# Other distances and pitches for the high and low parts of x, y and u in a two-layer encoder kernel

## The chip, the cores and the metric

The kernel runs on one core of one Trainium2 chip. The metric is the device time of one execution in microseconds; 2368.82 us is the median of three runs before the change (2368.69 to 2369.4). A second, profiled execution left the trace from which all rows below come.

## What is computed

Two encoder layers over 272 positions (256 tokens and 16 learned meta tokens) of width 2048. Each layer makes one wide projection, runs a gated linear attention and a neighbourhood attention side by side, projects their joined outputs back, and ends with a squared-ReLU MLP; two normalisations follow the two halves. Cut to its frame, the reference is:

```python
def _layer(h, w_in, ..., w_out, ln1_w, ln1_b, w_ff1, w_ff2, ln2_w, ln2_b):
    proj = jnp.einsum('bld,dp->blp', h, w_in)
    ...
    y_gla = _gla_mixer(gq, gk, gv, gr, glr, gla_w_up, gla_b_up, gla_norm_w)
    y_na = _na_mixer(nq, nk, nv, na_rel_bias).astype(h.dtype)
    mix = jnp.einsum('blm,md->bld', jnp.concatenate([y_gla, y_na], axis=-1), w_out)
    h = _layer_norm(DEEPNORM_ALPHA * h + mix, ln1_w, ln1_b)
    ff = jnp.einsum('blf,fd->bld', jnp.square(jax.nn.relu(jnp.einsum('bld,df->blf', h, w_ff1))), w_ff2)
    return _layer_norm(DEEPNORM_ALPHA * h + ff, ln2_w, ln2_b)
```

All is float32. Four products with weights carry nearly all the work: `w_in` (2048 x 6176), `w_out` (2048 x 2048), `w_ff1` (2048 x 8192) and `w_ff2` (8192 x 2048), in each layer.

## The kernel before

Each float32 factor is split into a high part, rounded to the matmul's float32r type, and a low part, which is what the rounding left. A product is made of three matmuls into one accumulator: high weights by high activations, high weights by low activations, and low weights by high activations. Positions are the columns of the moving operand, 128 channels at a time are the partitions. Layer 0 works on 272 positions; the last parts of layer 1 on 256.

**Activations.** A chunk is 128 channels of an activation, and a `Pair` (line 43) holds its two parts in one tile of the on-chip memory. `x` has 16 chunks and is the layer's input, `y` has 16 and is the attention's output. The MLP's hidden half, `u`, has 32 chunks: the first sixteen are laid over `y`'s tiles, the other sixteen (`u16` to `u31`) are in a pool of their own (line 788). A tile is `[P, 2, PITCH]`, PITCH = 288 elements: the high part starts at element 0 and the low part at 288, and the next chunk's tile follows 576 elements (2304 bytes) on. The tiles of `x` and `y` serve other uses at times: gate weights (line 373), the normalisation's rows and the outputs (`reuse`, line 938), the low part of the attention's values (line 294). Those read the tile as one flat row.

**Weights.** They stream from memory in tiles of 128 x 1024 (`made`, line 170): a DMA into `raw`, a copy on ScalarE to `wh` (line 178), a subtraction on VectorE to `wl` (line 179), each with three buffers. One tile holds eight stationary blocks of 128 x 128.

**Products.** `by_m` (line 248) makes one output tile of 128 channels at a time. For every eight chunks it calls `eight` (line 202), which multiplies them with one weight tile. Where there are 272 columns, line 214 gives for each chunk the high and then the low part to the same block of `wh`, sixteen matmuls, and line 217 then gives the eight high parts to `wl`. Where there are 256 columns (`once`), line 211 passes both parts of a chunk in one matmul of 2 x 256 columns, with an access pattern that jumps from the high part to the low part, eight matmuls, and line 217 follows with eight of 256 columns. A few products carry two columns more (258 and 274). `by_k` (line 228, matmuls in line 244) makes four or eight output tiles at once, two chunks at a time; it is used where chunks become ready one by one, and there the same part of a chunk is given to four blocks of weights running.

Matmuls run in the order in which they are issued. The rest of the work (gates, linear attention, neighbourhood attention, normalisation) is cut into generators, and `pump` (line 119) issues pieces of them between the products' groups. The change touches no order of this kind.

Of the kernel before, what the change touches and what calls it, by code (L numbers as in the profile page):

```python
# [7 lines left out]
F32 = mybir.dt.float32  # L8
F32R = mybir.dt.float32r
# [5 lines left out]
P = 128  # L15
D = 2048
DC = D // P
T = 256
# [4 lines left out]
GH, GDK, GDV = 4, 128, 256  # L23
# [14 lines left out]
MEET = 2  # L38
PAD = 40
PITCH = 288  # L40


class Pair(tuple):


    def __new__(cls, both):
        made = super().__new__(cls, (both[:, 0, :], both[:, 1, :]))
        made.both = both
        return made


class Trunk:
# [149 lines left out]
    def eight(self, ps, wh, wl, x, n, first, last, once):  # L202

        mm = self.nc.tensor.matmul
        c = lambda w, j: w[:, j * P:j * P + P]
        for j, v in enumerate(x):
            if once:  # L210
                mm(ps, lhsT=c(wh, j), rhs=v.both[:, :, :T], start=first and not j, stop=False)  # L211
                continue
            for i in range(2):
                mm(ps[:, :n], lhsT=c(wh, j), rhs=v[i][:, :n], start=first and not i + j, stop=False)  # L214
        o = ps[:, T:] if once else ps[:, :n]
        for j, (h, _) in enumerate(x):
            mm(o, lhsT=c(wl, j), rhs=h[:, :T if once else n], start=False, stop=last and j == 7)  # L217
# [55 lines left out]
        self.nc.vector.tensor_tensor(dst[low:low + n], src, dst[high[0]:high[0] + n].bitcast(F32), ALU.subtract)  # L273

    def pair(self, pool, name, c):
        return Pair(pool.tile([P, 2, PITCH], F32R, name=f"{name}{c}", tag=f"{name}{c}", bufs=1))


    def layer(self, l):
        nc, tc = self.nc, self.tc  # L280
        self.l = l
        self.full = l + 1 < DEPTH
        self.n = n = L if self.full else T
        with ExitStack() as actx:
            pool = lambda name, side, ctx=actx, bufs=1: ctx.enter_context(
                tc.tile_pool(name=name, bufs=bufs, side=side, reuse_waits="tile"))
            a = pool("att", "left")
            t = lambda nm, s: a.tile(s, F32, name=nm, tag=nm)
            self.qk = [t(f"qk{h}", [P, 2, L]) for h in range(GH)]
            for h in range(GH) if l else ():  # L290
                nc.gpsimd.memset(self.qk[h][:, 1, T:], 0.0)
            self.decay = [t(f"dec{h}", [P, 2, L]) for h in range(GH)]
            self.V = a.tile([P, 2 * GH, 2, P], F32R, name="V", tag="V")
            self.vlow = [self.pair(self.yp, "y", 12 + h).both.rearrange("p a c -> p (a c)") for h in range(GH)]
            self.VS = a.tile([80, GH * GDV], F32R, name="VS", tag="VS")
            nc.gpsimd.memset(self.VS.bitcast(F32), 0.0)
            self.y, self.gate, self.done, self.vt = [None] * DC, {}, set(), []
            if l:
                self.load_gates()
                self.by_m(self.x, [L + 2] * 4, lambda m, ps: self.fixed(self.ev_k, m, ps), pump=(1, NORMS[0]),  # L300
                          renew=True)
                first = self.by_k(self.x, L, self.normed)
                self.drain()
                self.lctx.close()
            with ExitStack() as ectx:
                self.ep = pool("early", "right", ectx)
                self.fcredit = 0
                self.fg.append(self.gates())
                if l == 0:
                    with ExitStack() as xctx:  # L310
                        self.xr = pool("xr", "right", xctx)
                        first = self.by_k(self.x, L, self.load_x, wide=True)
                    for m in range(4):
                        self.ev_k(m, first.pop(0))
                for m, ps in enumerate(first):
                    self.ev_v(m, ps)
                self.credit, self.alone = 0, True
                self.by_m(self.x, [n] * 4, self.ev_q, pump=(1, 1, True))
                self.by_m(self.x, [L] * 4, lambda m, ps: self.ev_v(4 + m, ps), pump=(1, 1, True))
                self.drain()  # L320
            self.a2 = pool("na", "left", bufs=2)
            with ExitStack() as gctx:
                self.credit = 0
                self.g2 = pool("gla", "right", gctx, 2)
                for h in range(GH):
                    self.bg.append(self.gla_head(h))
                for g in range(2):
                    self.by_m(self.x, [n] * 4, lambda m, ps: self.ev_r(4 * g + m, ps), pump=(1, GLA_R))
                self.na_tiles()
                for g in range(6):  # L330
                    if g == 5:
                        while self.bg:
                            self.step(self.bg, 1)
                        gctx.close()
                        self.ln_open()
                    ns = [n if (4 * g + m) % 3 == 0 else L for m in range(4)]
                    self.by_m(self.x, ns, lambda m, ps: self.ev_na(4 * g + m, ps), pump=(1, GLA_NA, True))
            self.alone = False
            ps = self.by_k(self.y, n, self.mixed)
            self.drain()  # L340
        self.tail(ps)
# [28 lines left out]

    def load_gates(self):

        place = lambda c: self.yp.tile([P, 2, PITCH], F32, name=f"gw{c}", tag=f"y{c}", bufs=1).rearrange("p a c -> p (a c)")[:, :512]
        *self.wup, self.wlr = (place(c) for c in (8, 9, 10))
        for d, w in enumerate(self.wup):
            self.nc.sync.dma_start(w[:LRK], self.i["wup"][self.l, :, d])
        self.nc.sync.dma_start(self.wlr, self.i["wlr"][self.l])
# [559 lines left out]

    def reuse(self, name, c, dtype):

        t = self.xp.tile([P, 2, PITCH], dtype, name=f"{name}{c}", tag=f"x{c}", bufs=1)  # L940
        return t.rearrange("p a c -> p (a c)")[:, :512]

    def affine(self, l, which, k):
        return tuple(self.vec[:, l, o:o + 1] for o in (32 * which + k, 32 * which + DC + k))
# [230 lines left out]
```

## Time and profile before

| what | value |
|---|---|
| median of three runs | 2368.82 us |
| profiled execution | 2369.49 us |
| its span | 2367.7 us |
| matmul instructions in the trace | 18180 |
| moved from memory | 414.03 MB |

The profile's page lists busy times by engine (PE is TensorE, PEld its weight load, DVE VectorE, ACT ScalarE, POOL GpSimd), slices of the span, the chain of work that ended last, and groups of instructions by line. In a group's row the fields are line, engine, operation, output tile and input tiles, shapes, count, then busy microseconds and the mean duration of one in nanoseconds, and behind the second bar the idle time before it with its releaser. A row of the timeline gives the start, the time that the merged instructions cover, and their count. Matmuls overlap: the time that one costs is the distance to the next one's start, and not its duration.

### The profile page before, as it was taken

Reading aid. Unit: us, or ns where it says so; the run is one execution under the profiler, and the core shown is the slowest. Engines: PE = TensorE matmul, PEld = TensorE weight load, DVE = VectorE, ACT = ScalarE, POOL = GpSimd, SP = SyncE. Lnnn points to the kernel's source line nnn. Section 1 sums busy time; section 2 is a strip of 40 time slices with the busy share of each in tenths; the row PEclk is TensorE's granted clock in tenths of the full one; section 3 lists DMA queues with packets and bytes.
Section 4 is the critical chain, followed back from the end, with each engine's and each line's share of the span. In section 5 each row is a group of like instructions: output and inputs, shape, how many; then the busy total and the mean of one; then the engine's idle time right before and its main releaser. Section 6 shows DMA issues by size and latency. Waiting matters only on the chain.

```text
span 2367.7 us, 44607 instructions
## 1 busy us (share of the span) xinstructions
PE 2359.4 (100%) x18180; PEld 2241.3 (95%) x18180; DVE 1520.6 (64%) x2432; ACT 1220.3 (52%) x2100; POOL 136.0 (6%) x200
## 2 busy tenths in 40 slices
PE   9999999999999999999999999999999999999998
PEld 9999999999999999999999899999988888888888
DVE  5588777775544455546576887778765455666654
ACT  5666664564433344444456666655644333444443
POOL 0021100100000000000030111101100000000000
PEclk9999999999999999999999999999999999999999
DMA  8555545555555556555555555456666666667664
GB/s 259 154 161 153 156 136 175 173 176 178 178 178 174 176 177 178 178 178 177 175 183 173 164 162 163 153 162 187 188 191 187 188 187 188 188 189 218 188 187 143
DMA packets 118301, 419.02 MB, mean 177 GB/s; under 512 B 13512, under 2 KB 14024, under 8 KB 118096
## 3 DMA queue, kind: packets, MB, share of 16 engines
q1 hardware_dynamic: 117808, 415.65, 57.7%
q8 instruction: 142, 2.33, 0.4%
q10 hardware_dynamic: 288, 0.52, 0.1%
q14 instruction: 63, 0.52, 0.1%
HBM read 414.03 MB, written 2.10 MB: 176 GB/s over the span
## 4 chain that ended last, share of the span: by engine, by line
PE 98%; DVE 1%; issue 0%; ACT 0%; POOL 0%; DVEq 0%; ACTq 0%; POOLq 0%
PE mm L214 35%; PE mm L217 29%; PE mm L211 22%; PE mm L244 6%; PE bg L244 1%; PE bg L754 1%; PE mm L693 1%; PE bg L554 0%; PE bg L400 0%; DVE wl L179 0%; PE mm L719 0%; PE mm L443 0%; PE bg L880 0%; PE bg L605 0%; PE bg L635 0%
## 5 line engine op out<-in xcount | busy, mean ns | idle before, releaser
L179 DVE TENSOR_TENSOR wl<-raw,wh 128x1024 fp32r<-128x1024 f32 (+1 forms) x768 | 941.9, 1227 | 625.3 <-ACT wh L178 622.2
L178 ACT CAST wh<-raw 128x1024 fp32r<-128x1024 f32 (+1 forms) x768 | 804.6, 1048 | 926.5 <-PE mm L214 381.2
L214 PE MATMUL mm<-x,wh 128*128 128x272 f32 (+2 forms) x4224 | 569.7, 287 | 0.0
L214 PEld LDWEIGHTS mm<-x,wh 128*128 128x128 f32 x4224 | 541.0, 188 | 0.8 <-PE mm L693 0.2
L217 PE MATMUL mm<-x,wl 128*128 128x272 f32 (+3 forms) x3264 | 466.3, 285 | 0.0
L217 PEld LDWEIGHTS mm<-x,wl 128*128 128x128 f32 x3264 | 436.9, 188 | 12.7
L211 PE MATMUL mm<-x,wh 128*128 128x512 f32 x1152 | 292.1, 396 | 0.0
L211 PEld LDWEIGHTS mm<-x,wh 128*128 128x128 f32 x1152 | 207.5, 189 | 38.4 <-PE mm L693 0.4
L217 PE MATMUL mm<-y,wl 128*128 128x272 f32 (+1 forms) x1408 | 200.0, 284 | 0.0
L217 PEld LDWEIGHTS mm<-y,wl 128*128 128x128 f32 x1408 | 189.0, 188 | 7.4
L214 PE MATMUL mm<-y,wh 128*128 128x272 f32 (+1 forms) x1440 | 193.3, 286 | 0.0
L214 PEld LDWEIGHTS mm<-y,wh 128*128 128x128 f32 x1440 | 184.3, 188 | 0.0
L211 PE MATMUL mm<-y,wh 128*128 128x512 f32 x688 | 174.3, 395 | 0.0
L217 PE MATMUL mm<-u,wl 128*128 128x272 f32 (+1 forms) x1024 | 145.4, 284 | 0.0
L211 PEld LDWEIGHTS mm<-y,wh 128*128 128x128 f32 x688 | 123.9, 189 | 22.4
L217 PEld LDWEIGHTS mm<-u,wl 128*128 128x128 f32 x1024 | 137.5, 188 | 5.4
L214 PE MATMUL mm<-u,wh 128*128 128x272 f32 (+1 forms) x1056 | 141.2, 286 | 0.0
L214 PEld LDWEIGHTS mm<-u,wh 128*128 128x128 f32 x1056 | 134.8, 188 | 0.0
L211 PE MATMUL mm<-u,wh 128*128 128x512 f32 x496 | 125.4, 395 | 0.0
L211 PEld LDWEIGHTS mm<-u,wh 128*128 128x128 f32 x496 | 89.4, 189 | 16.3
L244 PE MATMUL mm<-x,wh 128*128 128x272 f32 (+1 forms) x512 | 73.5, 289 | 0.0
L244 PEld LDWEIGHTS mm<-x,wh 128*128 128x128 f32 x512 | 68.0, 191 | 0.0
(273 smaller groups left out, 1857.2 us busy)
## 6 DMA issues: line engine op xcount, KB each, us to landing
raw<-in_wff SPq DMA_DIRECT2D x512, 512.0 KB, 3.6
raw<-in_win SPq DMA_DIRECT2D x190, 512.0 KB, 3.9
raw<-in_wout SPq DMA_DIRECT2D x64, 512.0 KB, 3.7
nb<-in_nab SPq DMA_DIRECT2D x16, 352.0 KB, 5.7
xraw<-in_xT SPq DMA_DIRECT2D x7, 272.0 KB, 4.7
out<-out SPq DMA_DIRECT2D x5, 256.0 KB, 3.2
brow<-in_norm SPq DMA_DIRECT2D x4, 256.0 KB, 4.9
gw<-in_wup SPq DMA_DIRECT2D x4, 196.0 KB
```

Of the source, the lines that this page charges most:

```text
L178: nc.scalar.copy(wh[:, c], raw[:, c])
L179: self.wl = nc.vector.tensor_tensor(wl[:, c], raw[:, c], wh[:, c].bitcast(F32), ALU.subtract).ins
L211: mm(ps, lhsT=c(wh, j), rhs=v.both[:, :, :T], start=first and not j, stop=False)
L214: mm(ps[:, :n], lhsT=c(wh, j), rhs=v[i][:, :n], start=first and not i + j, stop=False)
L217: mm(o, lhsT=c(wl, j), rhs=h[:, :T if once else n], start=False, stop=last and j == 7)
L244: self.nc.tensor.matmul(ps[g + m][:, :n], lhsT=parts[p][0][:, c:c + P], rhs=acts[k + j][parts[p][1]][:, :n], start=k + j + p == 0, stop=k ...
L693: nc.tensor.matmul(ps[hh][:, t * NKEY:t * NKEY + NKEY], lhsT=q[hs, NM + t * P:NM + t * P + P], rhs=k[hs, t, :], start=True, stop=True)
L754: nc.tensor.matmul(po[t][hs, :P], lhsT=v2[ts, hs] if rest else v1[:, t, hs], rhs=p2[ts, hh, :] if rest else p1[:, 2 * hh + t, :], start=re ...
```

## The change

Every group of tiles gets a distance between high and low part and a pitch of its own, in elements:

| tiles | distance, pitch before | distance, pitch after | in bytes after |
|---|---|---|---|
| x | 288, 576 | 288, 592 | 1152, 2368 |
| y (and u0 to u15) | 288, 576 | 288, 608 | 1152, 2432 |
| u16 to u23 | 288, 576 | 272, 576 | 1088, 2304 |
| u24 to u31 | 288, 576 | 320, 640 | 1280, 2560 |
| sp (sums of the normalisations) | 288, 576 | 288, 576 | 1152, 2304 |

The tile becomes one flat row; a `Pair` takes its parts as slices of it and makes the two-part view of line 211 once (`once`). The larger tiles need some 5 KB more on each partition, and the scratch for DMA descriptors goes from 8192 to 2048 bytes a partition.

```diff
+LAYOUT = {"x": (288, 592), "y": (288, 608), "u": (272, 576), "v": (320, 640), "sp": (288, 576)}
...
-    def __new__(cls, both):
-        made = super().__new__(cls, (both[:, 0, :], both[:, 1, :]))
-        made.both = both
+    def __new__(cls, flat, low):
+        width = min(low, flat.shape[-1] - low)
+        made = super().__new__(cls, (flat[:, :width], flat[:, low:low + width]))
+        made.flat, made.once = flat, flat[:, :2 * low].rearrange("p (a c) -> p a c", a=2)[:, :, :T]
         return made
...
-                mm(ps, lhsT=c(wh, j), rhs=v.both[:, :, :T], start=first and not j, stop=False)
+                mm(ps, lhsT=c(wh, j), rhs=v.once, start=first and not j, stop=False)
...
     def pair(self, pool, name, c):
-        return Pair(pool.tile([P, 2, PITCH], F32R, name=f"{name}{c}", tag=f"{name}{c}", bufs=1))
+        low, whole = LAYOUT["v" if name == "u" and c > 23 else name]
+        return Pair(pool.tile([P, whole], F32R, name=f"{name}{c}", tag=f"{name}{c}", bufs=1), low)
...
-            self.vlow = [self.pair(self.yp, "y", 12 + h).both.rearrange("p a c -> p (a c)") for h in range(GH)]
+            self.vlow = [self.pair(self.yp, "y", 12 + h).flat for h in range(GH)]
...
-        place = lambda c: self.yp.tile([P, 2, PITCH], F32, name=f"gw{c}", tag=f"y{c}", bufs=1).rearrange("p a c -> p (a c)")[:, :512]
+        place = lambda c: self.yp.tile([P, LAYOUT["y"][1]], F32, name=f"gw{c}", tag=f"y{c}", bufs=1)[:, :512]
...
-        t = self.xp.tile([P, 2, PITCH], dtype, name=f"{name}{c}", tag=f"x{c}", bufs=1)
-        return t.rearrange("p a c -> p (a c)")[:, :512]
+        return self.xp.tile([P, LAYOUT["x"][1]], dtype, name=f"{name}{c}", tag=f"x{c}", bufs=1)[:, :512]
...
-    nc = bacc.Bacc("TRN2", target_bir_lowering=False, num_devices=1, dynamic_dma_scratch_size=8192)
+    nc = bacc.Bacc("TRN2", target_bir_lowering=False, num_devices=1, dynamic_dma_scratch_size=2048)
```

Below, a chunk's "place" is the byte address of a part's first column within a partition, modulo 256.

## The prediction

> **What bounds the kernel now.** I read the page's first part, then the chain of waits, then the timeline of TensorE (PE).
>
> ```profile
> span 2367.7 us, 44607 instructions
> PE 2359.4 (100%) x18180; PEld 2241.3 (95%) x18180; DVE 1520.6 (64%) x2432; ACT 1220.3 (52%) x2100; POOL 136.0 (6%) x200
> PEclk9999999999999999999999999999999999999999
> PE 98%; DVE 1%; issue 0%; ACT 0%; POOL 0%; DVEq 0%; ACTq 0%; POOLq 0%
> PE mm L214 35%; PE mm L217 29%; PE mm L211 22%; PE mm L244 6%; PE bg L244 1%; PE bg L754 1%; PE mm L693 1%; PE bg L554 0%; PE bg L400 0%; DVE wl L179 0%; PE mm L719 0%; PE mm L443 0%; PE bg L880 0%; PE bg L605 0%; PE bg L635 0%
> L179 DVE TENSOR_TENSOR wl<-raw,wh 128x1024 fp32r<-128x1024 f32 (+1 forms) x768 | 941.9, 1227 | 625.3 <-ACT wh L178 622.2
> ```
>
> PE is idle for 2367.7 - 2359.4 = 8.3 us, at full granted clock in every slice, and four lines of matmuls (214, 217, 211, 244) are 93% of the chain. VectorE, which makes the low halves of the weights, stands idle 625 us waiting for ScalarE's high halves. So the kernel's time is the spacing from one matmul's start to the next, times their number, and nothing else moves it by much. A duration in the groups (287 ns) is no spacing, since matmuls overlap; the spacings come from the starts in the timeline. First layer 0, then layer 1:
>
> ```profile
> 600.63 1.16 PE L217 MATMUL mm<-x,wl 128*128 128x272 f32 x8
> 601.63 2.14 PE L214 MATMUL mm<-x,wh 128*128 128x272 f32 x16
> 603.61 1.16 PE L217 MATMUL mm<-x,wl 128*128 128x272 f32 x8
> 604.61 1.65 PE L214 MATMUL mm<-x,wh 128*128 128x272 f32 x12
> ```
> ```profile
> 2000.40 2.02 PE L211 MATMUL mm<-x,wh 128*128 128x512 f32 x8
> 2002.26 1.11 PE L217 MATMUL mm<-x,wl 128*128 128x256 f32 x8
> 2003.21 1.09 PE L211 MATMUL mm<-x,wh 128*128 128x512 f32 x4
> ```
>
> L214: (603.61 - 601.63) / 16 = 123.75 ns for 272 columns. L217: (604.61 - 603.61) / 8 = 125.0 ns for 272 columns, (2003.21 - 2002.26) / 8 = 118.75 ns for 256. L211: (2002.26 - 2000.40) / 8 = 232.5 ns for 2 x 256. The change alters nothing but where these matmuls' moving operands lie, so I ask whether the place shows in a spacing.
>
> **What place does so far.** In bytes the old distance is 1152 = 4 x 256 + 128 and the old pitch 2304 = 9 x 256. So every high part starts at the same place of 256 bytes (call it 0) and every low part at 128. L214 reads high, low, high, low (0, 128, 0, 128); L217 reads eight high parts, always starting at 0. L244 reads one chunk's part four times running, and another group reads from other places altogether: lines 635 to 637 read pieces of a packed tile whose starts lie 1088 = 4 x 256 + 64 bytes apart. From the chain of waits in order of time, and from the timeline:
>
> ```profile
> 494.24 24.10 PE mm L244 x192
> 1680.23 22.83 PE mm L244 x192
> ```
> ```profile
> 312.12 0.29 PE L636 MATMUL bg<-parts,V 128*128 128x272 f32 x1
> ...
> 313.64 0.29 PE L639 MATMUL bg<-am,VS 80*128 80x272 f32 x1
> ```
> ```profile
> 600.63 0.28 PE L217 MATMUL mm<-x,wl 128*128 128x272 f32 x1
> ...
> 600.75 0.54 PE L217 MATMUL mm<-x,wl 128*128 128x272 f32 x3
> ...
> 600.88 0.54 PE L217 MATMUL mm<-x,wl 128*128 128x272 f32 x3
> ```
>
> L244 makes 24.10 / 192 = 125.5 ns at 272 columns, 22.83 / 192 = 118.9 ns at 256. The mixed places make (313.64 - 312.12) / 12 = 126.7 ns (twelve spacings between first and last row). So at 272 columns repeating a start costs 125.0 to 125.5, alternating 0 and 128 costs 123.75: some 1.75 ns. At 256 columns there is no such difference. Within one L217 group single spacings differ: 600.63 to 600.75 is 120 ns, 600.75 to 600.88 is 130 ns. The same instruction on the same kind of tile can be 10 ns cheaper, so there is something to win, and 120 ns is the best that these rows show.
>
> The floor lies lower. The kernel's first four real matmuls are (5.46 - 4.55) / 4 = 228 ns apart:
>
> ```profile
> 4.55 1.11 PE L244 MATMUL mm<-x,wh 128*128 128x272 f32 x4
> 5.46 0.66 PE L244 MATMUL mm<-x,wl 128*128 128x272 f32 x2
> ```
>
> If the array runs there at half its later rate, 114 ns would be the price of the columns alone (an estimate), and 10 of the 123.75 ns would be overhead. The Trainium skill's page "TensorE: Matmul & The Clock Gate", section "Back-to-back issue gap", gives N/2.4 + 2.5 ns for a warm matmul, 115.8 ns at 272 columns; the trace's 123.75 is 8 ns above that, and by that rule alone no choice of addresses would be worth anything.
>
> **The change part by part.** The instructions of each engine stay the same in number, form and order; addresses move. The counts, by form:
>
> ```profile
> L214 PE MATMUL mm<-x,wh 128*128 128x272 f32 x3584 | 483.0, 287 | 0.0
> L211 PE MATMUL mm<-x,wh 128*128 128x512 f32 x1152 | 292.1, 396 | 0.0
> L217 PE MATMUL mm<-x,wl 128*128 128x272 f32 x1792 | 260.3, 287 | 0.0
> L214 PE MATMUL mm<-y,wh 128*128 128x272 f32 x1408 | 189.2, 286 | 0.0
> L211 PE MATMUL mm<-y,wh 128*128 128x512 f32 x688 | 174.3, 395 | 0.0
> L217 PE MATMUL mm<-x,wl 128*128 128x256 f32 x1152 | 159.8, 281 | 0.0
> L214 PE MATMUL mm<-u,wh 128*128 128x272 f32 x1024 | 137.1, 286 | 0.0
> L211 PE MATMUL mm<-u,wh 128*128 128x512 f32 x496 | 125.4, 395 | 0.0
> L217 PE MATMUL mm<-y,wl 128*128 128x272 f32 x704 | 102.3, 287 | 0.0
> L217 PE MATMUL mm<-y,wl 128*128 128x256 f32 x704 | 97.7, 281 | 0.0
> L217 PE MATMUL mm<-x,wl 128*128 128x274 f32 x192 | 28.2, 289 | 0.0
> L217 PE MATMUL mm<-x,wl 128*128 128x258 f32 x128 | 18.0, 283 | 0.0
> ```
>
> In the built program x, y and u lie at different multiples of 256 bytes, yet their groups of one form agree within 1 ns, so I count places modulo 256 alone. The new places are: x high 0, 64, 128, 192 from chunk to chunk, low 128 further; y high 0, 128, 0, 128, low 128 further; the first eight chunks of u high 0, low 64; the last eight high 0 and low 0.
>
> *L217 and its 274- and 258-column kin, on x and y:* consecutive starts no longer repeat. No row has a run of starts that all step by 64 or 128. Bounds: 120 ns (best single spacing) and 126.7 ns (mixed places). I take the middle between 125.0 and 120, 122.5 ns, since the best spacings occur in this very form: -2.5 ns x (1792 + 704 + 192 + 128 = 2816) = -7.0 us; bounds -14.1 and +4.8 us. At 256 columns repetition cost nothing, so 0 for 1152 + 704; bounds 1 ns either way, 1.9 us. On u the high parts still repeat: 0.
>
> *L211:* on x and y a matmul no longer starts where its forerunner did: -2.5 ns x (1152 + 688 = 1840) = -4.6 us. For u, where the jump to the low part also becomes 64 or 0 instead of 128, I take 0. Bounds: two separate 256-column matmuls, 237.5 ns, which is +5.0 ns; and 256 columns more at the slope of L217, (125.0 - 118.75) / 16 = 0.39 ns, which is 218.7 ns or -13.8. For 2336 matmuls that is +11.7 to -32 us.
>
> *L214:* on x each start still differs from the one before: 0. On y the low part of a chunk and the high part of the next now start at the same place, so half of 1408 pay the repetition: 704 x 1.75 = +1.2 us. On the first eight of u: 0. On the last eight every start repeats: 512 x 1.75 = +0.9 us. Bounds for 6016 matmuls: 120 ns, -22.6 us, and 126.7 ns, +17.7 us.
>
> *L244:* four matmuls running read the same part, so starts repeat as before: 0, bounds 1.75 ns on about 960, 1.7 us either way.
>
> *Everything else* costs nothing. ScalarE and VectorE write the parts at other addresses under PE's cover; the first would have to grow by the 625 us that VectorE waits to be felt. The scratch for descriptors that shrinks is used by no queue here (all are hardware queues):
>
> ```profile
> q1 hardware_dynamic: 117808, 415.65, 57.7%
> q10 hardware_dynamic: 288, 0.52, 0.1%
> ```
>
> Sum: -7.0 - 4.6 + 1.2 + 0.9 = -9.5 us. The profiled execution took 2369.49 us (span 2367.7 and 1.8 around it), so 2360.0; it is 0.7 above the median of 2368.82, so **2359 us** for a median. If PE gains 9.5 us, the weights must come 0.4% faster; VectorE's wait shows room, so no other engine is late next.
>
> **The rivals.** *Slower.* A 272-column stream ends 64 bytes past its starting place (1088 = 4 x 256 + 64). In L214 every next stream now begins 64 bytes beyond that end, after high as after low; that relation, and not alternation as such, may make the 123.75. After the change it survives only for high to low in x and y. If the rest fall to the mixed 126.7, L214 as a whole loses up to 17.7 us, and L217 and L211, which go from one untuned relation to another, give half of my gain, 5.8: +11.9, about 2381 us. It decides from 11.6 / 6016 = 1.9 ns per L214 matmul on. For it: L214 is the cheapest of the four groups at 272 columns, and that relation is what it has to itself. Against it: the 126.7 was measured on a tile that the built program puts 32 bytes off a multiple of 64, which no new place is.
>
> *Nothing.* Every old and new distance is a multiple of 64 bytes. If only the place within 64 matters, nothing changes: 2369 us. For it: at 256 columns all groups make 118.75 to 118.9. Against it: 123.75 beside 125.0. The Trainium skill's page "SBUF — State Buffer", section "Who interferes with whom", says the same more strongly: PE and ScalarE "never wait on anyone" and the moving operand and the weights have a read port each. By that rule the time stays; 120 and 130 ns within one group of rows speak against it.
>
> *Much faster.* All 272-column matmuls reach 120 ns and L211 loses the same 3.5 ns: -14.1 - 22.6 - 8.2 = -45 us, 2324 us. For it: 120 ns occurs. Against it: groups average it away everywhere today.
>
> **How the numbers follow.** Forecast 0.51, slower 0.27, nothing 0.12, much faster 0.10. The forecast's own range, half the way to each bound, the terms added as independent, is 2340 to 2372. The range that holds 8 in 10 goes from 2333, short of the much faster case, to 2382, the slower one. About 0.2%, 4.7 us, is what a measurement tells from no change. Faster by more: 0.10 and most of 0.51, together 0.58; within: 0.12 and 0.03 of the forecast's edge, 0.15; slower: 0.27.
>
> **What would show it.** Right: L217 at 272 columns on x near 122.5 ns where it was 125.0, L211 on x near 230, L214 on x still 123.75, on the last eight of u 125.5. Wrong: L217 on x at 125 or above; L214 on x at 125 or more (then the slower rival); all groups as before (nothing). A PE idle for more than 8.3 us would show that something other than spacings moved.

## The result and the profile after

The changed kernel takes 2372.93 us (median of 20 runs) where the one before takes 2369.03 (20 runs beside them): a ratio of 1.0016, interval 1.001 to 1.0022. It is 3.9 us slower, inside the 0.2% that was set as no change, but clear of the noise, and on the other side from the forecast of 9.5 us faster. The profile's page of the changed kernel; code lines lie two further down, and three from line 277 to line 939:

```profile
span 2371.1 us, 44606 instructions
PE 2362.8 (100%) x18180; PEld 2242.4 (95%) x18180; DVE 1520.3 (64%) x2432; ACT 1219.3 (51%) x2100; POOL 136.4 (6%) x200
PEclk9999999999999999999999999999999999999999
PE mm L216 35%; PE mm L219 29%; PE mm L213 22%; PE mm L246 6%; PE bg L246 1%; PE bg L757 1%; PE mm L696 1%; PE bg L557 0%; PE bg L403 0%; DVE wl L181 0%; PE mm L722 0%; PE mm L446 0%; PE bg L883 0%; PE bg L608 0%; PE bg L638 0%
L181 DVE TENSOR_TENSOR wl<-raw,wh 128x1024 fp32r<-128x1024 f32 (+1 forms) x768 | 941.9, 1227 | 628.3 <-ACT wh L180 627.1
```

TensorE is idle for 2371.1 - 2362.8 = 8.3 us, as before, at full granted clock, with the same chain and the same count of matmuls. The 3.4 us that the span grew are all in the spacings of matmuls. From the timeline of the changed kernel, x in layer 0, then in layer 1, then u and y in layer 0 (start, time covered, line, count); the last block is u and y before the change:

```profile
601.42 1.16 PE L219 MATMUL mm<-x,wl 128*128 128x272 f32 x8
602.41 2.15 PE L216 MATMUL mm<-x,wh 128*128 128x272 f32 x16
604.40 1.16 PE L219 MATMUL mm<-x,wl 128*128 128x272 f32 x8
605.39 0.78 PE L216 MATMUL mm<-x,wh 128*128 128x272 f32 x5
```
```profile
2000.21 1.10 PE L219 MATMUL mm<-x,wl 128*128 128x256 f32 x8
2001.15 2.03 PE L213 MATMUL mm<-x,wh 128*128 128x512 f32 x8
2003.02 1.10 PE L219 MATMUL mm<-x,wl 128*128 128x256 f32 x8
```
```profile
644.19 2.16 PE L216 MATMUL mm<-u,wh 128*128 128x272 f32 x16
646.19 1.17 PE L219 MATMUL mm<-u,wl 128*128 128x272 f32 x8
647.19 2.17 PE L216 MATMUL mm<-u,wh 128*128 128x272 f32 x16
649.20 1.16 PE L219 MATMUL mm<-u,wl 128*128 128x272 f32 x8
650.20 2.17 PE L216 MATMUL mm<-y,wh 128*128 128x272 f32 x16
652.21 1.16 PE L219 MATMUL mm<-y,wl 128*128 128x272 f32 x8
```
```profile
643.35 2.14 PE L214 MATMUL mm<-u,wh 128*128 128x272 f32 x16
645.33 1.16 PE L217 MATMUL mm<-u,wl 128*128 128x272 f32 x8
646.33 2.14 PE L214 MATMUL mm<-u,wh 128*128 128x272 f32 x16
648.31 1.16 PE L217 MATMUL mm<-u,wl 128*128 128x272 f32 x8
649.31 2.14 PE L214 MATMUL mm<-y,wh 128*128 128x272 f32 x16
651.29 1.16 PE L217 MATMUL mm<-y,wl 128*128 128x272 f32 x8
```

On x, in the groups shown, L219 at 272 columns falls from 125.0 to (602.41 - 601.42) / 8 = 123.75 ns and at 256 from 118.75 to (2001.15 - 2000.21) / 8 = 117.5; L213 rises from 232.5 to (2003.02 - 2001.15) / 8 = 233.75; L216 rises from 123.75 to (604.40 - 602.41) / 16 = 124.4. On the first eight of u L216 takes (646.19 - 644.19) / 16 = 125.0, on the last eight and on y (652.21 - 650.20) / 16 = 125.6; before, L214 took (645.33 - 643.35) / 16 = 123.75 on all three. Gains and losses of one nanosecond nearly cancel. Over the whole trace, each matmul's distance to the next start, averaged by line (numbers of before), tiles and columns:

```
line tiles columns   count   before  after ns   sum of differences us
211  x     2x256      1152   233.23  234.23    +1.15
211  y     2x256       688   232.49  232.77    +0.20
211  u16-23, u24-31    496   232.50  233.43, 230.10   +0.23, -0.59
214  x     272        3584   124.61  125.05    +1.61
214  y     272        1408   123.94  125.59    +2.32
214  u16-23, u24-31   1024   123.73  125.12, 125.41   +0.70, +0.88
217  x     272        1792   126.02  125.20    -1.47
217  y     272         704   125.09  124.97    -0.08
217  x     256        1152   119.45  118.42    -1.19
217  y     256         704   118.40  117.10    -0.92
217  u16-23, u24-31 256  512   118.37  119.64, 119.10   +0.33, +0.18
all others                                     -0.05
sum                                            +3.3
```

(The averages of x hold the few waits at the start of a product, which are nearly the same before and after.)

### The profile page after: what moved, and what is told of

Read it like the earlier page. It is cut to its first block, busy times and chain, and to the rows that moved or that the text cites. A ratio compares the mean times of both kernels' runs of the same rounds, so it can differ in the third digit from the quotient of the medians.

```text
span 2371.1 us, 44606 instructions
## 1 busy us (share of the span) xinstructions
PE 2362.8 (100%) x18180; PEld 2242.4 (95%) x18180; DVE 1520.3 (64%) x2432; ACT 1219.3 (51%) x2100; POOL 136.4 (6%) x200
## 4 chain that ended last, share of the span: by engine, by line
PE 98%; DVE 1%; issue 0%; ACT 0%; POOL 0%; DVEq 0%; ACTq 0%; POOLq 0%
PE mm L216 35%; PE mm L219 29%; PE mm L213 22%; PE mm L246 6%; PE bg L246 1%; PE bg L757 1%; PE mm L696 1%; PE bg L557 0%; PE bg L403 0%; DVE wl L181 0%; PE mm L722 0%; PE mm L446 0%; PE bg L883 0%; PE bg L608 0%; PE bg L638 0%
## 5 line engine op out<-in xcount | busy, mean ns | idle before, releaser
L216 PE MATMUL mm<-x,wh 128*128 128x272 f32 (+2 forms) x4224 | 571.2, 287 | 0.0
L216 PEld LDWEIGHTS mm<-x,wh 128*128 128x128 f32 x4224 | 541.3, 188 | 0.8 <-PE mm L696 0.2
L219 PE MATMUL mm<-x,wl 128*128 128x272 f32 (+3 forms) x3264 | 464.0, 284 | 0.0
L219 PEld LDWEIGHTS mm<-x,wl 128*128 128x128 f32 x3264 | 434.7, 188 | 13.1
L213 PE MATMUL mm<-x,wh 128*128 128x512 f32 x1152 | 293.3, 396 | 0.0
L213 PEld LDWEIGHTS mm<-x,wh 128*128 128x128 f32 x1152 | 206.7, 188 | 39.6 <-PE mm L696 0.4
L219 PE MATMUL mm<-y,wl 128*128 128x272 f32 (+1 forms) x1408 | 199.0, 283 | 0.0
L216 PE MATMUL mm<-y,wh 128*128 128x272 f32 (+1 forms) x1440 | 195.6, 287 | 0.0
L219 PEld LDWEIGHTS mm<-y,wl 128*128 128x128 f32 x1408 | 188.2, 188 | 7.5
L216 PEld LDWEIGHTS mm<-y,wh 128*128 128x128 f32 x1440 | 186.3, 188 | 0.0
L213 PE MATMUL mm<-y,wh 128*128 128x512 f32 x688 | 174.4, 395 | 0.0
L219 PE MATMUL mm<-u,wl 128*128 128x272 f32 (+1 forms) x1024 | 146.1, 285 | 0.0
L213 PEld LDWEIGHTS mm<-y,wh 128*128 128x128 f32 x688 | 123.1, 188 | 22.9
L219 PEld LDWEIGHTS mm<-u,wl 128*128 128x128 f32 x1024 | 138.3, 189 | 5.4
L216 PE MATMUL mm<-u,wh 128*128 128x272 f32 (+1 forms) x1056 | 142.8, 287 | 0.0
L216 PEld LDWEIGHTS mm<-u,wh 128*128 128x128 f32 x1056 | 136.1, 188 | 0.0
L213 PE MATMUL mm<-u,wh 128*128 128x512 f32 x496 | 125.0, 394 | 0.0
L213 PEld LDWEIGHTS mm<-u,wh 128*128 128x128 f32 x496 | 89.0, 188 | 16.3
```

Source lines behind the costliest of these rows:

```text
L213: mm(ps, lhsT=c(wh, j), rhs=v.once, start=first and not j, stop=False)
```

## The experiments

All run the reference's computation but for the three that are named. "Spacing" is as above, start to next start, from each run's own trace.

### One group of tiles at a time

```diff
-LAYOUT = {"x": (288, 592), "y": (288, 608), "u": (272, 576), "v": (320, 640), "sp": (288, 576)}
+LAYOUT = {'x': (288, 592), 'y': (288, 576), 'u': (288, 576), 'v': (288, 576), 'sp': (288, 576)}
```

and in the same way for y, for the first eight own chunks of u, and for the last eight.

> x alone gets the new pitch (288, 592); y and u keep 288, 576; the descriptor scratch is small as in the changed kernel. Theory A (the spacing of a matmul depends on the places of its own group's starts modulo 256 bytes): only the spacings of x move, as they did in the changed kernel: 272 columns in L216 124.6 to 125.05 ns, in L219 down by 0.8 ns, 256 columns down by 1 ns, 2 x 256 up by 1 ns; sum of the differences about 0, so 2369. Theory B (something that all groups share, the smaller scratch or the shift of everything behind it, makes the change): about +3.9 us here too, 2373, and y and u slower though their distances are old.

> y alone gets (288, 608). Theory A: y at 272 columns in L216 goes from 123.9 to 125.6 ns (1408 matmuls, +2.3 us), y at 256 in L219 from 118.4 to 117.1 (-0.9), 2 x 256 +0.2: +1.5 us, 2370.5; x and u as before. Theory B: about 2373 with x and u changed.

> The first eight own chunks of u alone get (272, 576). Theory A: their 512 matmuls at 272 columns in L216 go from 123.75 to 125.1 ns (+0.7 us), 256 columns +0.3, 2 x 256 +0.2: +1.3 us, 2370.3; the last eight as before. Theory B: about 2373.

> The last eight chunks of u alone get (320, 640). Theory A: 272 columns in L216 123.7 to 125.4 (+0.9 us), 256 columns +0.2, 2 x 256 from 232.5 to 230.1 (-0.6): +0.5 us, 2369.5, inside the noise; the four kernels' differences add up to the whole change. Theory B: about 2373.

Measured beside one set of runs before (2369.13 us): x 2369.38 (ratio 1.0001, 0.9992 to 1.001), y 2370.93 (1.0009, 1.0 to 1.0018), the first eight of u 2370.99 (1.0008, 0.9999 to 1.0017), the last eight 2370.57 (1.0007, 0.9998 to 1.0016). Single ratios hardly leave the noise; the spacings do, since a group that a run leaves alone repeats closely: with x alone, no group of y or u on these three lines moved by more than 0.03 us in all. With y alone, x (old places) and then y (new places), from the timeline:

```profile
601.46 2.14 PE L216 MATMUL mm<-x,wh 128*128 128x272 f32 x16
603.44 1.16 PE L219 MATMUL mm<-x,wl 128*128 128x272 f32 x8
...
649.21 2.17 PE L216 MATMUL mm<-y,wh 128*128 128x272 f32 x16
651.22 1.15 PE L219 MATMUL mm<-y,wl 128*128 128x272 f32 x8
```

x keeps (603.44 - 601.46) / 16 = 123.75 ns, y has (651.22 - 649.21) / 16 = 125.6 as in the changed kernel. Summed over each trace, the spacings' differences are -0.4 us (x), +1.3 (y), +2.3 (first eight), +1.3 (last eight), 4.5 together, and the medians' differences 0.25 + 1.8 + 1.86 + 1.44 = 5.35, where the whole change has 3.3 and 3.9.

Theory B falls: no single group brings the whole change, and with x alone y and u stay. Theory A holds for x, and only in part for the others: a group also changes its neighbours. With y alone, untouched L216 of the first eight of u goes from 123.75 to 125.0 ns (+0.6 us), and with the last eight alone, untouched L216 of y from 123.94 to 124.52 (+0.8 us). With the first eight alone, their own L216 goes to 126.0 ns, where the whole change has 125.1, and the untouched last eight go from 123.7 to 124.2; that is most of why the first eight cost 2.3 us and not the expected 1.3, and y's +0.8 is why the last eight cost 1.3 and not 0.5. All are products over 32 chunks, in which y and u follow each other. Effects of this size are enough for the four not to add up.

### Other addresses, the same places

```diff
-LAYOUT = {"x": (288, 592), "y": (288, 608), "u": (272, 576), "v": (320, 640), "sp": (288, 576)}
+LAYOUT = {'x': (288, 576), 'y': (288, 576), 'u': (352, 704), 'v': (352, 704), 'sp': (288, 576)}
```

> All sixteen own chunks of u get distance 352 and pitch 704 (1408 = 5 x 256 + 128 and 2816 = 11 x 256 bytes): other addresses, the old places modulo 256. Theory A (places modulo 256 alone): every spacing of u as before, 272 columns in L216 123.7 ns, 2 x 256 232.5, 256 columns 118.4; 2369. Rival C (the distance itself or a larger modulus counts): u's spacings move by 1 to 2 ns as with (272, 576) and (320, 640), +1 to +3 us.

2368.97 us beside 2369.01 (ratio 1.0, 0.9991 to 1.0009), and the sum of spacings of u moved by 0.00 us. For u's old places, then, neither the distance as such nor the address beyond 256 bytes counts; the smaller scratch, which this kernel has too, does not either. C falls here.

### Matmuls alone

A kernel of its own with 32 matmuls running per block and a fixed step between starts (the `one` below), blocks parted by one short matmul; then blocks of 2 x 256 columns with a distance and a step. The encoder is left out; the output is a copy of the input.

```python
ONE = [(n, step, twice, wp) for n, steps in ((272, (1280, 1344, 1152, 1216, 1088)), (256, (1280, 1344, 1152, 1216, 1024)))
       ...
def one(nc, ps, w, m, n, at, j, wp, k):
    nc.tensor.matmul(ps[:, :n], lhsT=w[:, wp + j * P:wp + j * P + P], rhs=m[:, at:at + n], start=not k, stop=k == REP - 1)
```

> Matmuls alone, no other engine at work: 32 running with one step between starts, then the next step; the encoder is left out and the output is a copy of the input. If consecutive places modulo 256 set the spacing: 272 columns with step 0 modulo 256 (1280 bytes) about 125, with 64 or 128 about 123 to 124, with 192 between; 256 columns 118 and 117. If the other engines' traffic makes the overhead over the columns' own 113 ns, all steps fall to about 114 to 116 at 272 columns and 107 to 110 at 256.

The busy time of each engine between 32 and 180 us, then the timeline of two blocks:

```profile
32.00:180.00 148.00, 148.00 (x930) 134.27 (x929) 0.00 (x0) 0.00 (x0) 0.00 (x0) 1.00 0.00 1
```
```profile
32.05 0.19 PE L31 MATMUL acc<-m,w 128*128 128x64 f32 x1
32.08 4.20 PE L22 MATMUL acc<-m,w 128*128 128x272 f32 x32
36.11 0.19 PE L31 MATMUL acc<-m,w 128*128 128x64 f32 x1
36.14 4.25 PE L22 MATMUL acc<-m,w 128*128 128x272 f32 x32
40.23 0.19 PE L31 MATMUL acc<-m,w 128*128 128x64 f32 x1
```

In the first row only TensorE and its weight loads are busy (the three zeros are VectorE, ScalarE and GpSimd; clock 1.00, DMA 0.00). The block with step 1152 takes 36.11 - 32.05 = 4.06 us. The next differs only in that two matmuls running take the same weights: 40.23 - 36.11 = 4.12 us. Spacings of the last sixteen of a block: at 272 columns 126.7 ns for step 0, 125.0 for 64, 123.4 for 128, 125.9 for 192; at 256 columns 120.0, 117.5, 118.3 and 118.4, and again 120.0 for step 1024, which is also 0. For 2 x 256 columns, over the last eight, from 228.1 ns (distance 0, step 0) to 234.5, and distances 1024 and 1280 agree within 0.1 ns. At 272 columns step 0 is dearest and 128 cheapest, as expected; the 114 to 116 ns of the other expectation do not occur. The overhead thus needs no other engine and no transfer: it is TensorE with itself. The Trainium skill's page "TensorE: Matmul & The Clock Gate", section "Back-to-back issue gap", gives N/2.4 + 2.5, an estimate of 115.8 ns at 272 columns, for an isolated matmul, not for a stream of weight loads and matmuls, and no address; no block here comes near it.

The places modulo 256 do not settle every spacing of these blocks. A step of 1088 bytes, which is 64 modulo 256 like 1344, took 125.8 ns and not 125.0. And the block in which two matmuls running share their weights has the steps and the weights' places of the one before it, yet took 125.0 ns and not 123.4; L214 of the old kernel, which also gives each block of weights to two matmuls with steps of 1152 bytes, took 123.75.

### Sixteen layouts

The eight-chunk product itself, with its two weight tiles, four calls per layout, once with 272 columns (16 + 8 matmuls) and once with 2 x 256 and 256 (8 + 8). The encoder is left out; the output is a copy of the input.

```python
LOWS, PITCHES = (1280, 1088, 1152, 1216), (2560, 2624, 2688, 2752)
...
            rhs = m[:, at:at + 2 * low].rearrange("p (a c) -> p a c", a=2)[:, :, :256]
            nc.tensor.matmul(ps, lhsT=wh[:, j * P:j * P + P], rhs=rhs, start=first and not j, stop=False)
```

> Four calls of the eight-chunk product for each of 16 layouts (distance and pitch at 0, 64, 128, 192 modulo 256 bytes), once with 272 columns and once with 2 x 256 and 256; the encoder is left out. Theory A: the order of layouts is the one of the whole kernel: 272 columns, distance 128 pitch 0 (the old layout) cheapest at about 372 ns a chunk, (128, 64) 374, (128, 128), (64, 0) and (0, 0) about 375; at 256 columns (0, 0) and (128, 128) 349.5 to 350, old 351, (128, 64) 351.5, (64, 0) 353. Rival: no order like it, the kernel's differences come from its other engines' traffic.

Nanoseconds for all matmuls of one chunk, from the second call's start to the fourth's, divided by 16 chunks:

```
                 272 columns, pitch mod 256      256 columns, pitch mod 256
distance mod 256    0     64    128    192          0     64    128    192
     0            375.8  376.7  375.0  377.2      349.2  350.0  347.5  350.9
    64            377.5  376.7  373.3  374.6      353.4  350.0  350.9  349.2
   128            373.0  372.5  375.8  375.0      350.8  350.8  350.8  350.0
   192            376.8  375.0  375.8  375.7      350.0  349.2  350.0  350.8
```

The order is nearly the expected one, but (128, 64) at 272 columns came out cheaper than the old layout, where it was put dearer. The old layout (128, 0) is still among the cheapest three there. Of the new ones, x's (128, 64) is 0.5 cheaper, y's (128, 128), the first eight's (64, 0) and the last eight's (0, 0) 2.8, 4.5 and 2.8 dearer; at 256 columns they are 0, 0, +2.6 and -1.6. With half of L214's counts, 1792, 704, 256 and 256 chunk products at 272 columns, and 248 for each half of u at 256, that is -0.9 + 2.0 + 1.2 + 0.6 + 0.7 - 0.4 = +3.2 us against the +3.3 of the trace. The sum owes part of its closeness to luck: x at 272 columns is -0.9 here and +0.1 in the trace (L214 and L217 together), y at 256 columns is 0 here and -0.7 in the trace. For the other terms the two agree within 0.4 us. So the table gives the loss of the whole kernel from TensorE alone, with an error of about 1 us for a group.

### Where the weights lie

```diff
+        self.yp.tile([P, 16], F32, name="shift", tag="shift")
         self.wp = pool("wst", bufs=3)
```

with the old distances and pitches. The tile of 64 bytes lies ahead of y, so y, the weights and u all move by 64 bytes, and x alone stays.

> All distances and pitches are the old ones; the weights' buffers lie 64 bytes further. Theory D (what counts is the place of the moving stream relative to the weights that are loaded meanwhile): the cheap pattern becomes dear, L216 at 272 columns from 123.75 to about 126.7 ns, and the repeated start cheap, L219 at 272 columns from 125.0 to about 123.3: 6016 x 2.9 - 3008 x 1.7 = +12 us, 2381. Rival (only the starts of moving streams to each other count): nothing moves, 2369.

> Matmuls alone, 272 and 256 columns, start steps of 0, 64, 128, 192 modulo 256 by weights at 0, 64, 128, 192; with weights at 64 also all starts 64 further. The encoder is left out and the output is a copy of the input. Theory D: starts 64 further with weights at 64 repeat the spacings of weights at 0 exactly; weights at 64 alone turn step 128 from 123.4 to 126.7 ns at 272 columns. Rival: the weights' place changes nothing.

The whole kernel takes 2371.39 us beside 2369.01 (ratio 1.0011, 1.0002 to 1.002). The 12 us were reckoned as if x, y and u all stayed; y and u did not, and that made a better control. Timeline, x and then u and y (L217 and L220 are L214 and L217 of the old kernel):

```profile
599.90 2.17 PE L217 MATMUL mm<-x,wh 128*128 128x272 f32 x16
601.90 1.16 PE L220 MATMUL mm<-x,wl 128*128 128x272 f32 x8
...
644.85 2.14 PE L217 MATMUL mm<-u,wh 128*128 128x272 f32 x16
646.83 1.16 PE L220 MATMUL mm<-u,wl 128*128 128x272 f32 x8
...
650.81 2.14 PE L217 MATMUL mm<-y,wh 128*128 128x272 f32 x16
652.79 1.16 PE L220 MATMUL mm<-y,wl 128*128 128x272 f32 x8
```

u and y moved together with the weights and keep 1.98 / 16 = 123.75 ns; summed over the trace their spacings moved by -0.01 and -0.02 us. x stayed where it was, so that its place relative to the weights changed, and its L214 went to (601.90 - 599.90) / 16 = 125.0 ns here, 126.1 over all, from 124.6: +5.4 us, of which its other lines gave 3.5 back. The rival, by which nothing moves, falls. The 1.5 ns are half of the 2.9 that were expected.

Alone, as the last 16 spacings of a block (encoder left out, output a copy of the input):

```
start step modulo 256:            0      64     128    192
272 columns, weights at 0       125.25 125.0  123.31 126.5
272, weights and starts at 64   125.44 125.0  123.31 125.81
272, weights alone at 64        123.31 125.81 125.38 125.88
272, weights alone at 128       126.69 125.0  125.0  125.81
272, weights alone at 192       126.69 125.0  126.69 125.69
256 columns, weights at 0       120.0  117.5  118.31 118.38
256, weights and starts at 64   120.0  117.5  118.75 118.31
256, weights alone at 64        117.75 118.31 116.69 118.31
256, weights alone at 128       118.81 117.5  118.75 118.31
256, weights alone at 192       117.75 117.5  117.75 118.31
```

Moving both together leaves most spacings alone (0.7 ns at the most); moving the weights alone makes the repeated start the cheap one at 272 columns (123.3) and the alternating one dear (125.4; 126.7 in the kernel of steps). With both at the old relation, step 0 gave 125.25 ns here and 126.7 in the kernel of steps, so a difference of 1.4 ns between two rows proves little; those of 2 to 3 ns at steps 0 and 128 go beyond it. Theory D holds in its main point: what counts is where the moving stream lies relative to the weights. That the loading of the next weights, which runs meanwhile, is what it meets fits the rows and is not shown by itself. The Trainium skill's page "SBUF — State Buffer", section "Who interferes with whom", gives the two an independent read port each and lets TensorE wait for nobody; these rows depend on the two places together, and the measurement decides.

### A version that beats both

```diff
+LAYOUT = {"x": (288, 640), "y": (288, 576), "u": (288, 576), "sp": (288, 576)}
+LATE = {"x": 320, "y": 256, "u": 256}
...
+        made.flat, made.once = flat, bass.AP(flat.tensor, flat.offset + at, [flat.ap[0], [low, 2], [1, T]])
...
+        return Pair(t, LATE[name], c % 2 * 32) if late else Pair(t, low)
```

`late` holds in the last layer for y, for u and for the MLP's x: places that the table has as (0, 128), the cheapest at 256 columns, while everything that is read with 272 columns keeps (128, 0).

> The old places wherever there are 272 columns; in the last layer y, u and the MLP's x, which are read with 256 columns alone, get a distance of 0 and starts alternating 0, 128 modulo 256. Theory A with the spacings of the 16 layouts: a chunk's two matmuls fall from 350.8 to 347.5 ns, on 832 of x, 688 of y and 496 of u: 2016 x -3.3 = -6.6 us, 2362.4, below both kernels. Rival: the sequence in the whole kernel does not settle as it does alone, and the gain is lost: 2369.

2360.64 us beside 2369.01: a ratio of 0.9965, 0.9951 to 0.9978, 8.4 us faster than before (the changed kernel had 2372.93 in its own runs). Timeline (L214 and L220 are L211 and L217 of the old kernel):

```profile
1989.71 2.00 PE L214 MATMUL mm<-x,wh 128*128 128x512 f32 x8
1991.55 1.09 PE L220 MATMUL mm<-x,wl 128*128 128x256 f32 x8
1992.48 2.00 PE L214 MATMUL mm<-x,wh 128*128 128x512 f32 x8
```

(1991.55 - 1989.71) / 8 = 230.0 ns instead of 232.5, (1992.48 - 1991.55) / 8 = 116.3 instead of 118.75. Over the trace the sum is -9.0 us: 2 x 256 columns -5.2, 256 columns -3.1, and the rest elsewhere, most of it (-0.6) in L244 on x, which differs by as much between runs that leave its places alone. A table of one product, measured alone, forecast the kernel's gain as 6.6 us.

## Why the prediction was wrong

Where the change acts was right: on spacings of TensorE alone, through the places of its operands, with no other engine and no wait taking part. What the places do was not: the rule that a repeated start is dear and a changed one cheaper gave the wrong size to each large term, and the sum turned its sign.

- **L217 on x and y, -7.0 us.** This step failed. It took 122.5 ns, the middle between the repeated start's 125.0 and the best single spacing, for starts that no longer repeat. Measured over 272, 274 and 258 columns: -1.3 us. A best single spacing is followed by a worse one: the eight of the old L217 on x run 121, 134, 125, 122, 124, 127, 124, 124 ns in a typical group, so the 120 and the 130 that the prediction read are one pair, and 120 ns was no price that a whole group could have.
- **L211 on x and y, -4.6 us.** The same 2.5 ns were carried over to a form without a row for it. Measured +1.35 us: x is 1 ns dearer, y 0.3. On u, where 0 was put, it was -0.4. The sixteen layouts show no rule of "do not repeat" at 256 columns: distance 0 with pitch 0, where everything repeats, is cheaper than the old layout.
- **L217 at 256 columns, 0.** Measured -1.6 us over x, y and u, and -2.1 on x and y, just outside the bound of 1.9. L217 and L244 both had 119 ns, and that made places look indifferent there; alone, steps move it from 117.5 to 120.0 ns.
- **L214, +2.1 us.** Measured +5.3. The last eight of u came out as reckoned (0.9 and 0.88). y lost 2.3 and not 1.2, and not where it was reckoned: from a low part's start to the next high part's, which now share a place, the distance stayed (126.1 before, 125.9 after), and from high to low, where the step is the old one, it rose from 121.9 to 125.3. x lost 1.4 where 0 was put, the first eight of u 0.7.
- **L244 and everything else, 0.** Right: -0.2 us for L244, nothing elsewhere.
- **The rivals.** The slower one was right in its place, L214 loses because the old layout is a good one for it, but not in its size: 5.3 us of the 17.7, as none of the new layouts falls to 126.7 throughout. Its reason, the step from one stream's end to the next one's start, is not enough either: with the weights alone moved, the same steps of 1152 bytes took 125.4 and 126.7 ns. "Nothing" named the time best, 2369 against 2372.93, by luck, for a reason that the experiments refute: steps of 0, 64, 128 and 192 bytes, all multiples of 64, differ by up to 3.3 ns at 272 columns. "Much faster" took single spacings for a group's price, as the forecast did.

In short, the prediction made a rule of the starts of consecutive streams from two groups of one kernel, and what holds is about the streams and the weights together. In the old kernel the weights and all high parts lie at the same place modulo 256, so the two could not be told apart there; the single spacings of 120 and 130 ns within a group of equal starts were the sign that something else takes part.

What stays open is how the two streams meet. The same block gave 126.7 ns in one kernel and 125.25 in another (272 columns, step 0, weights at 0), so it can settle in more than one pattern; steps of 1088 and 1344 bytes differ, and so does a block whose weights are used twice, though their places are the same; and the untouched neighbours of a changed group moved too. What came before thus takes part, and the places alone do not give a spacing. No run here shows which part of the memory or of TensorE makes the wait.

## What to carry to other kernels

Where TensorE runs without gaps on float32r operands, as here, the addresses of moving operand and weights modulo 256 bytes are worth something: between the sixteen layouts a chunk's matmuls differ by up to 1.7% (347.5 to 353.4 ns at 256 columns), and a choice made from them took 0.35% off the whole kernel. A layout that is good for one form of matmul is not good for another. Measure the very sequence of matmuls alone, over all places, and read the sum of a period: a table of that kind accounted for the loss after the event (+3.2 us against +3.3, in part by luck) and forecast the gain of the last kernel beforehand (6.6 us, measured 8.4), where reasoning from single spacings had the sign wrong. Put the layout that each stage likes into that stage, instead of one layout for a tile's whole life.

## What was not expected of the hardware

Matmuls of 272 float32r columns, with nothing else at work, have no constant spacing: at step 128 they alternate between 120 and 126 ns, at step 0 in one block between 125 and 128 or 129, at 256 columns and step 0 they keep 120 throughout. Such patterns go on to the end of a block, to within 1 ns; at step 192 no short one is seen, and in the changed kernel the groups of y and of the first eight of u fall into several. A jump within the access pattern costs nothing to be seen: in the last kernel 2 x 256 columns took 230.0 ns on the MLP's x, which jumps 320 elements, and 229.8 to 229.9 on u and y, whose parts follow without a gap.
